# A Strassen product for the second half of the tokens in a transformer-layer kernel, low parts on GpSimd, and paced loads

## The chip, the cores and the metric

The kernel runs on one core of a Trainium2 chip. Its engines work side by side, each through its own list of instructions in strict order: TensorE (PE in the profile; its weight loads are PEld), VectorE (DVE), ScalarE (ACT), GpSimd (POOL) and SyncE (SP), which here only issues DMA transfers. The metric is the device time of one execution in microseconds. Three runs of the kernel before took 1467.42 to 1470.21 us, median 1467.71.

## The reference

The kernel computes one transformer layer on x (1024 tokens x 1024 features, float32) and 256 memory tokens: token mixing by two kinds of attention heads, cross-attention into the memory, and a squared-ReLU MLP. Each step is normalised before and after and added to the residual. The change touches the cross-attention's output product, and the loads of the head outputs that feed the mixing's output product:

```python
    y = jnp.concatenate([rmsnorm(y_fox.reshape(B, S, D_FOX), g_fox_out[l]),
                         rmsnorm(y_chk.reshape(B, S, D_CHK), g_chk_out[l])], axis=-1)
    x = x + rmsnorm(y @ w_out[l], g_mix_post[l])
    h = rmsnorm(x, g_mem_pre[l])
    mem_n = rmsnorm(mem, g_mem_kv[l])
    y = memory_cross_attention(h, mem_n, w_mq[l], w_mk[l], w_mv[l], w_mo[l])   # (P V) reshaped @ w_mo
    x = x + rmsnorm(y, g_mem_post[l])
    h = rmsnorm(x, g_ff_pre[l])
    y = jnp.square(jax.nn.relu(h @ w_ff1[l])) @ w_ff2[l]
```

## The kernel before

**High and low parts.** Every float32 operand of a product is split into a high part (ACT copies it into the matmul's type) and a low part (a subtraction, on DVE mostly). `mm3` (L191) makes one product of three matmuls: high x high, high x low, low x high. A weight block is loaded into a raw tile (tag `wraw`, three buffers), split into the tags `whi` and `wlo` (home "w", two buffers), into `wq` (one further pair) or into general tiles `u4` (30 buffers), and used.

**The planner.** From the attention to the middle of the cross-attention the order of all instructions is written by a planner, `Flow` (L56). Steps of TensorE stand in several streams. In each round the first stream whose next step is ready gives its matmuls; work for ACT ("S"), DVE ("V"), GpSimd ("G") and SyncE ("D") is put into waiting lists with a start time, a cost and a level, and the lowest level that is due goes first. The planner's costs and landing times are guesses written into the code: a load takes 0.55 us on SyncE's queue and lands `took` us later, and work that needs it is planned for that moment. The chip then runs the lists in that order and waits wherever a guess was too short.

**Head outputs.** Each attention head stores its output in DRAM (`od`, L761, through two buffers `o`). `Outputs.one` (L1009) loads them back as `oin`, four tiles of 128 x 512 for each half of the tokens (`th`) and group of heads (`g`), L1044. ACT and DVE split them into yT_hi and yT_lo (L1038, L1039), and `mix_steps` (L1174) multiplies them by w_out. For g = 0 the loads of both halves are issued together with a landing time of 7.0; for g = 1 it is 4.0.

**Cross-attention.** `query_steps`, `memory_score_steps`, `memory_turn_steps` and `memory_out_steps` (L1411) run for both halves of the tokens, head by head. For the first half (th = 0) the output product with w_mo is made by Strassen's algorithm (Winograd's form) in `strassen_steps` (L1443): the 512 x 1024 x 1024 product is cut into 256-token and 512-feature blocks, and seven block products stand for eight. `operand_tiles`, `operand_parts` and `sum_parts` make the sums of blocks of the head outputs (A11, A12, A22, S1 to S4) with high and low parts; the sums of weight blocks (T1 to T4) are made once by `Sums` (L1088) and kept in DRAM (`td`). `strassen_leave` (L1484) adds the products up in the rows y. Its weight pairs are given the homes "w", "w", "wq" in turn. For the second half (th = 1) the product is plain: `product_steps` (L1530) makes the left 512 columns inside the planner, with four weight pairs in "w", and the right 512 columns are made behind the planner, in the part written by hand.

**The turn.** Behind the planner comes an order by hand (L1986 on). The four row blocks of the second half are finished: right half of the product (24 matmuls a row block), `row_out`, `row_sum`, `row_norm` (L1970 to L1984). Beside them stand the first feed-forward products `ahead(j)` (L1891, 24 matmuls each, weights split by `split_ahead`, L1883). `Turn` (L1914) transposes the normalised rows on TensorE (`turn`), makes the block sums of the feed-forward's own Strassen product (`sums`) and their low parts (`low`): T2, T1, T3, T4 and B22. Before the manual part GpSimd makes eight sums `xf` (L1907) of the first half's parts.

Of the kernel before, what the change touches and what calls it, by code (L numbers as in the profile page):

```python
# [55 lines left out]
class Flow:  # L56
# [18 lines left out]
    def load(self, at, call, then=None, took=4.5):  # L75
        self.put("D", at, 0.55, call, then and (lambda end: then(end + took)))
# [59 lines left out]
def build(ctx, tc, nc, out, t):  # L136
# [249 lines left out]
    class Stock:  # L386
# [3 lines left out]
        def __init__(self):  # L390
# [602 lines left out]
    class Outputs:  # L993
# [15 lines left out]
        def one(self, th, g):  # L1009
# [20 lines left out]
            for i in range(2):  # L1030
                for j in range(2):
# [12 lines left out]
                    flow.load(flow.now, lambda o=o, kc=kc: nc.sync.dma_start(o, od[kc][th]), loaded, 7.0 - 3 * g)  # L1044
# [291 lines left out]
    def operand_tiles(h):  # L1336

        k = h % 2
        if h < 2:
            opt["r", k] = u4(f"ro{k}", (P, 2, HT), F32)  # L1340
            spent["r", k] = all_of(("r spent", k), 2, free["u4"].give)
        for n in ("A11",) if h < 2 else ("A12", "A22"):
            opt[n, k] = u4(f"{n}o{k}", (P, 2, 2, Q))
        if h == 0:
            opt["S3"] = u4("S3o", (P, 2, 2, Q), F32)
            for n, i in [(n, i) for n in ("S1", "S2", "S3", "S4") for i in range(2)]:
                parts_of[n, i] = all_of(("all", n, i), 3, lambda at, n=n, i=i: sum_parts(n, i, at))
            hi_tiles(("S3",))
        if h == 2:
            opt["S4"] = u4("S4o", (P, 2, 2, Q), F32)  # L1350
            spent["S4"] = all_of(("S4 spent",), 2, free["u4"].give)

    def operand(n, i):

        return opt[n, i][:, 0], opt[n, i][:, 1]

    def sum_parts(n, i, at):
        x = opt[n][:, i] if n in ("S3", "S4") else opt["r", i][:, :, Q:] if n == "S1" else opt["r", i][:, :, :Q]
        hi, lo = operand(n, i)

        def then(end):
            seen["A", n, i] = end
            if n != "S3":
                spent["S4" if n == "S4" else ("r", i)](end)
# [4 lines left out]
    def hi_tiles(names):  # L1369

        for n in names:
            for k in range(2):
                opt[n, k] = u4(f"{n}o{k}", (P, 2, 2, Q))
                parts_of[n, k](flow.end)
# [3 lines left out]
    def operand_parts(h, nb, ps):  # L1378

        k = h % 2  # L1380
        L, R = (opt["r", k][:, nb, c] for c in (slice(0, Q), slice(Q, HT)))
        left = lambda at: free["pv"].give(at)
        if nb == 0:
            lows[h] = all_of(("A", "A11" if h < 2 else "A12", k), 2)
            lows[h, 1] = all_of(("A", "A22", k), 2)
        if h < 2:
            ah, al = opt["A11", k][:, 0, nb], opt["A11", k][:, 1, nb]
            s3 = opt["S3"][:, k, nb]
            flow.put("S", flow.end, 0.6, lambda: nc.scalar.activation(opt["r", k][:, nb, :], ps, AF.Copy),
# [3 lines left out]
                         flow.put("V", at, 0.42, lambda: nc.vector.tensor_sub(s3, L, R), parts_of["S3", k])))  # L1393
            return
        hi, lo = ([opt[n, k][:, x, nb] for n in ("A12", "A22")] for x in range(2))
        s4 = opt["S4"][:, k, nb]
        halves = (ps[:, :Q], ps[:, Q:])
        gone = all_of(("out read", h, nb), 2, left)

        def block(x, then, level):  # L1400
# [7 lines left out]
                   lambda at: (gone(at), [parts_of[n, k](at) for n in ("S2", "S1", "S4")]), 0)  # L1408
        block(1, lambda at: (gone(at), lows[h, 1](at)), 1)

    def memory_out_steps():  # L1411
        for th in range(2):
            for h in range(4):
                done = all_of(("o", th, h), 2)
                for nb in range(2):
                    yield 1.362, lambda: there(("pt", th, h, 0), ("pt", th, h, 1)) and free["pv"].ready() \
                        and (nb or free["u4"].ready(2 if th else OPERANDS[h]))
                    if nb == 0:
                        for _ in range(2 if th else OPERANDS[h]):
                            free["u4"].take()  # L1420
                        if th:
                            outs[th, h] = u4(f"oT_hi{th}{h}", (P, 2, HT)), u4(f"oT_lo{th}{h}", (P, 2, HT))
                        if not th:
                            operand_tiles(h)
# [6 lines left out]
                    if not th:  # L1431
                        operand_parts(h, nb, ps)
                        continue
                    oh, ol = (x[:, nb, :] for x in outs[th, h])
                    flow.put("S", flow.end, 0.6, lambda oh=oh, ps=ps: nc.scalar.activation(oh, ps, AF.Copy),
                             lambda at, oh=oh, ol=ol, ps=ps, done=done: flow.put(
                                 "V", at, 0.7, lambda: nc.vector.tensor_sub(ol, ps, f(oh)),
                                 lambda end: (free["pv"].give(end), done(end))))
# [4 lines left out]
    def strassen_steps():  # L1443
# [4 lines left out]
        for p, (an, bn) in enumerate(PRODUCTS):  # L1448
            for i in range(2):
                for b in range(2):  # L1450
                    def room():
# [5 lines left out]
                    yield (1.362, lambda: there(("mo", 0, bn, i), ("A", an, i)) and (i or (  # L1457
                        there(("sum", before, b)) if goes_on else room())))
# [1006 lines left out]
```

## Time and profile before

| what | value |
|---|---|
| median of three runs | 1467.71 us |
| profiled execution, its own time | 1468.91 us |
| span of that execution | 1467.1 us |
| granted TensorE clock, mean | 0.998 |
| TensorE busy | 1450.2 us |
| VectorE busy | 997.1 us |
| ScalarE busy | 822.0 us |
| GpSimd busy | 420.4 us |
| DMA moved | 232.17 MB, mean 158 GB/s |

Times in the profile are microseconds from the start of the span; "mean ns" is the mean duration of one instruction. Instructions on one engine overlap: the next starts before the one ahead has ended, so what an instruction costs an engine is read from starts that stand back to back, not from its duration. A bracket behind a row tells how long the engine was idle before it and what ended that. A row with x8 merges eight instructions that follow each other. SPq is SyncE's queue. In a row of a stretch (two times with a colon) stand the length, the busy times of PE, PEld, DVE, ACT and POOL with their counts, the granted clock, the share of the DMA engines, and GB/s. The output product of the first half runs from about 679 to 728 us, that of the second half from 795.4 to 845.8, the turn from there to about 888.

### The profile page before, as it was taken

Reading aid. Unit: us, or ns where it says so; the run is one execution under the profiler, and the core shown is the slowest. Engines: PE = TensorE matmul, PEld = TensorE weight load, DVE = VectorE, ACT = ScalarE, POOL = GpSimd, SP = SyncE. Lnnn points to the kernel's source line nnn. Section 1 sums busy time; section 2 is a strip of 40 time slices with the busy share of each in tenths; the row PEclk is TensorE's granted clock in tenths of the full one; section 3 lists DMA queues with packets and bytes.
Section 4 is the critical chain, followed back from the end, with each engine's and each line's share of the span. In section 5 each row is a group of like instructions: output and inputs, shape, how many; then the busy total and the mean of one; then the engine's idle time right before and its main releaser. Section 6 shows DMA issues by size and latency. Waiting matters only on the chain.

```text
span 1467.1 us, 21030 instructions
## 1 busy us (share of the span) xinstructions
PE 1450.2 (99%) x7265; PEld 1223.0 (83%) x7265; DVE 997.1 (68%) x1704; ACT 822.0 (56%) x1439; POOL 420.4 (29%) x518
## 2 busy tenths in 40 slices
PE   9999999999999999999999999999999999999997
PEld 8988888888889788888788888888888888888886
DVE  6787777767668756975874687765555666655576
ACT  7567777666677736555553455545555543444442
POOL 1245456545445201531231413343222000000020
PEclk9999999999999999999999999999999999999999
DMA  7132324321326494552541547764444785445565
GB/s 274 48 98 72 79 69 139 83 83 46 92 62 172 152 331 150 170 190 81 178 157 44 186 143 248 241 221 158 144 156 167 283 319 180 139 150 191 187 244 201
DMA packets 88986, 232.17 MB, mean 158 GB/s; under 512 B 10648, under 2 KB 14752, under 8 KB 88880
## 3 DMA queue, kind: packets, MB, share of 16 engines
q1 hardware_dynamic: 88736, 230.57, 47.8%
q8 instruction: 57, 0.93, 0.3%
q14 instruction: 49, 0.40, 0.1%
q10 hardware_dynamic: 144, 0.26, 0.1%
HBM read 167.30 MB, written 55.11 MB: 152 GB/s over the span
## 4 chain that ended last, share of the span: by engine, by line
PE 92%; DMA 3%; DVE 2%; ACT 1%; issue 1%; SPq 0%; POOL 0%; DVEq 0%; ACTq 0%; POOLq 0%
PE pv L754 4%; PE fx L194 4%; PE fx L193 4%; PE fx L195 4%; PE ptr L711 4%; PE px L195 3%; PE px L194 3%; PE fy L193 3%; PE fy L194 3%; PE px L193 3%; PE fy L195 3%; PE q L193 2%; PE mq L195 2%; PE q L195 2%; PE q L194 2%; PE pz L193 2%
## 5 line engine op out<-in xcount | busy, mean ns | idle before, releaser
L717 DVE TENSOR_TENSOR phl<-ptr,phl 128x512 fp32r<-128x512 f32 (+1 forms) x152 | 92.5, 616 | 31.8 <-ACT phl L720 31.0
L2162 ACT ACTIVATE whif<-ra 128x1024 fp32r<-128x1024 f32 x37 | 39.2, 1061 | 130.4 <-PE fy L194 62.6
L2164 DVE TENSOR_TENSOR wlof<-ra,whif 128x1024 fp32r<-128x1024 f32 x37 | 45.3, 1225 | 91.8 <-ACT whif L2162 91.8
L720 ACT ACTIVATE phl<-ptr 128x512 fp32r<-128x512 f32 (+1 forms) x152 | 79.8, 540 | 40.7 <-PE ptr L711 38.8
L2284 POOL TENSOR_SCALAR rf<-sf 128x1 f32<-128x1 f32 x7 | 7.9, 1129 | 321.7 <-ACT jf L2265 321.4
L754 PE MATMUL pv<-phl,vs 128*128 128x512 f32 (+1 forms) x304 | 85.3, 366 | 3.0 <-DVE phl L717 3.0
L754 PEld LDWEIGHTS pv<-phl,vs 128*128 128x128 f32 x304 | 55.0, 188 | 14.4 <-DVE phl L717 4.2
L768 POOL TENSOR_TENSOR o<-o 64x256 f32<-64x256 f32 x64 | 47.0, 734 | 68.6 <-DVE o L766 50.0
L195 PE MATMUL fx<-vhif,wlof 128*128 128x512 f32 x168 | 65.4, 389 | 0.0
L193 PE MATMUL fx<-vhif,whif 128*128 128x512 f32 x168 | 65.4, 389 | 0.0
L194 PE MATMUL fx<-vlof,whif 128*128 128x512 f32 x168 | 65.4, 389 | 0.0
L2049 POOL TENSOR_TENSOR sc<-wf,wf 128x512 f32<-128x512 f32 x14 | 21.5, 1535 | 142.1 <-DMA wf<-in_w_ff 97.6
L766 DVE TENSOR_TENSOR o<-pv,o 64x512 f32<-64x512 f32 x64 | 44.0, 688 | 18.2 <-ACT o L771 16.9
L193 PE MATMUL k<-hT_hi,whik 128*128 128x512 f32 x128 | 53.6, 419 | 0.0
L193 PE MATMUL yw<-whiwo,yT_hi 128*128 128x512 f32 x128 | 51.1, 399 | 2.0 <-ACT yw L1196 2.0
L193 PE MATMUL q<-hT_hi,whiq 128*128 128x512 f32 x128 | 51.6, 403 | 0.0
L193 PE MATMUL mq<-h2T_hi,whimq 128*128 128x512 f32 x128 | 51.2, 400 | 0.0
L194 PE MATMUL yw<-wlowo,yT_hi 128*128 128x512 f32 x128 | 50.6, 396 | 0.0
L771 ACT ACTIVATE o<-pv 64x512 f32<-64x512 f32 x64 | 38.0, 593 | 22.4 <-issue 6.4
L195 PE MATMUL yw<-whiwo,yT_lo 128*128 128x512 f32 x128 | 50.4, 394 | 0.0
L195 PE MATMUL k<-hT_hi,wlok 128*128 128x512 f32 x128 | 50.3, 393 | 0.0
L195 PE MATMUL mq<-h2T_hi,wlomq 128*128 128x512 f32 x128 | 50.1, 392 | 0.2 <-DVE wlomq L455 0.2
(696 smaller groups left out, 5034.3 us busy)
## 6 DMA issues: line engine op xcount, KB each, us to landing
ra<-gd SPq DMA_DIRECT2D x56, 512.0 KB, 3.9
wg<-in_w_ff SPq DMA_DIRECT2D x56, 512.0 KB, 5.6
wf<-in_w_ff SPq DMA_DIRECT2D x38, 512.0 KB, 3.9
gd<-s SPq DMA_DIRECT2D x48, 256.0 KB, 2.1
wrawmq<-in_w_mq SPq DMA_DIRECT2D x16, 512.0 KB, 3.9
gd<-u SPq DMA_DIRECT2D x32, 256.0 KB, 2.4
gd<-g SPq DMA_DIRECT2D x25, 256.0 KB, 2.2
wrawq<-in_w_qk SPq DMA_DIRECT2D x8, 512.0 KB, 4.8
```

Of the source, the lines that this page charges most:

```text
L193: nc.tensor.matmul(ps, lh, rh, start=start, stop=False, skip_group_check=more)
L194: nc.tensor.matmul(ps, lh, rl, start=False, stop=False, skip_group_check=more)
L195: nc.tensor.matmul(ps, ll, rh, start=False, stop=stop, skip_group_check=more)
L711: nc.tensor.transpose(tr[:, m, :], sp[:, k * P:(k + 1) * P], ident)
L717: flow.put("V", at, 0.7, lambda: nc.vector.tensor_sub(pl[:, live, :], tr[:, live, :], f(ph[:, live, :])), done)
L720: flow.put("S", flow.end, 0.6, lambda ph=ph, tr=tr, live=live: nc.scalar.activation(ph[:, live, :], tr[:, live, :], AF.Copy), split)
L754: nc.tensor.matmul(pv[:, :, qs_, :], v, hl[:, :, hs, :], start=c == 0 and turn == 0, stop=last)
L766: flow.put("V", at, 0.7, lambda: nc.vector.tensor_add(o2[own], pv[own, :, :, ::step], o2[own]), lambda end: (free["pv"].give(end), flow.pu ...
L768: free["pv"].give(end), flow.put("G", end, 0.8, lambda: nc.gpsimd.tensor_add(o2[own, 0], o2[own, 0], o2[own, 1]), store)))
L771: flow.put("S", flow.end, 0.6, lambda: nc.scalar.activation(o2[own], pv[oth, :, :, ::step], AF.Copy), both)
L2162: nc.scalar.activation(ah, ra, AF.Copy)
L2164: nc.vector.tensor_sub(al, ra, f(ah))
```

## The change

- The planner's `load` takes a level. The loads of the head outputs are put at level 1, behind other loads that are due. For g = 0 they start 1.6 us apart (the second half's from 6.4 us on). Their landing time is 6.0 for both groups.
- The second half's output product is Strassen's too. Its tables of operands, tiles and sums get `th` as a key. Its 14 weight pairs replace eight; ten of them have the home "w", and B22 and T4 (four pairs) go to `u4`.
- Products 1 to 5 of the second half run in the planner. The last two are made in the order by hand: the sixth goes on in the banks that the fifth left (`left_over`), the seventh into new ones. `row_out` now adds (or subtracts) the bank into the row before it squares and scales.
- `ahead(0)` stands in front of the first `turn`; `ahead(1)` and `ahead(2)` move up too, and the row sums and norms are placed anew.
- The residual rows are loaded into `u4` tiles, three of them at once.
- At the turn, the low parts of T3 and T4 and the second half of the low parts of the feed-forward weights from j = 3 on go from DVE to GpSimd.
- `product_steps` is gone.

```diff
-    def load(self, at, call, then=None, took=4.5):
-        self.put("D", at, 0.55, call, then and (lambda end: then(end + took)))
+    def load(self, at, call, then=None, took=4.5, level=0):
+        self.put("D", at, 0.55, call, then and (lambda end: then(end + took)), level)
...
-                self.blocks += [(("mo", th, nh, kp), row_pair(t["w_mo"], kp, nh), pair)
-                                for nh in range(2) for kp in range(4)] if th else [
-                    (("mo", 0, b, i), row_pair(t["w_mo"], where[b][0] + i, where[b][1]) if b in where else td[b][i], pair)
+                self.blocks += [
+                    (("mo", th, b, i), row_pair(t["w_mo"], where[b][0] + i, where[b][1]) if b in where else td[b][i], pair)
                     for _, b in PRODUCTS for i in range(2)]
...
-                    if b[0][:3] == ("mo", 1, 1):
+                    if b[0][:3] in (("mo", 1, "B22"), ("mo", 1, "T4")):
                         self.home[b[0]] = "u4"
...
-                    flow.load(flow.now, lambda o=o, kc=kc: nc.sync.dma_start(o, od[kc][th]), loaded, 7.0 - 3 * g)
+                    flow.load(flow.now + 1.6 * (kc % 4 + 4 * th) * (1 - g), lambda o=o, kc=kc: nc.sync.dma_start(
+                        o, od[kc][th]), loaded, 6.0 if g == 0 else 6.0, 1)
...
     def second_filler():
         yield from mix_steps(0)
         yield from mix_steps(1)
         yield from query_steps(0)
-        yield from strassen_steps()
+        yield from strassen_steps(0)
         yield from query_steps(1)
-        yield from product_steps(1, (0,))
+        yield from strassen_steps(1, 5)
...
-            was[j] = HiLo(raw, D, wp, "w", 2, f"a{j}").both(nc.vector)
+            h = was[j] = HiLo(raw, D, wp, "w", 2, f"a{j}")
+            if j < 3:
+                h.both(nc.vector)
+                return
+            h.split_hi()
+            for e, cs in ((nc.vector, slice(0, HT)), (nc.gpsimd, slice(HT, D))):
+                e.tensor_sub(h.lo[:, cs], raw[:, cs], f(h.hi[:, cs]))
...
-            return lambda: nc.vector.tensor_sub(l, s, f(h))
+            return lambda: (nc.gpsimd if n in ("T3", "T4") else nc.vector).tensor_sub(l, s, f(h))
...
     def residual_in(b):
-        xts[b] = p2.tile([P, D], F32, tag="xt", bufs=2, name=f"xth3{4 + b}")
+        xts[b] = u4(f"xth3{4 + b}", (P, D), F32)
         nc.sync.dma_start(xts[b], x1d[4 + b])

     def row_out(b, ps):
-        square_sum(ps, ss[b][:, 1:2], HT)
-        nc.vector.tensor_tensor(y[b][:, HT:], ps, gmpost[:, HT:], op=ALU.mult)
+        cs = slice(HT, D) if b < 2 else slice(0, HT)
+        c, n = y[b][:, cs], cs.start // HT
+        if b < 2:
+            nc.vector.tensor_add(c, ps, c)
+        else:
+            nc.vector.tensor_sub(c, c, ps)
+        square_sum(c, ss[b][:, n:n + 1], HT)
+        nc.vector.tensor_tensor(c, c, gmpost[:, cs], op=ALU.mult)
         rx[b] = inverse_rms(ss[b][:, 0:1], f"h3y{4 + b}", ss[b][:, 1:2])
...
-    residual_in(0)
     raws = {}
-    for b in range(4):
-        c = slice(b * P, (b + 1) * P)
-        ps = mm_tile([P, HT], f"ym11{b}", "tr" if b < 2 else "pv")
-        for kp in range(4):
+    for b in range(3):
+        residual_in(b)
+
+    def last_product(b):
+        an, bn = PRODUCTS[5 if b < 2 else 6]
+        ps = left_over[4, b] if b < 2 else mm_tile([P, HT], f"ym16{b}", ("tr", "pv")[b % 2])
+        c = slice(b % 2 * P, (b % 2 + 1) * P)
+        for i in range(2):
+            (oh, ol), (wh, wl) = operand(1, an, i), stock.w["mo", 1, bn, i]
             for j in range(2):
-                mm3(ps, o[kp][0][:, j, c], o[kp][1][:, j, c], wo[kp][0][:, j, :], wo[kp][1][:, j, :],
-                    kp == 0 and j == 0, kp == 3 and j == 1)
-        if b:
-            row_sum(b - 1)
-            row_norm(b - 1)
-        if b < 3:
-            raws[EARLY + b] = ff1_raw(EARLY + b)
-            residual_in(b + 1)
-            row_out(b, ps)
+                mm3(ps, oh[:, j, c], ol[:, j, c], wh[:, j, :], wl[:, j, :],
+                    b > 1 and i == 0 and j == 0, i == 1 and j == 1, b < 2)
+        return ps
...
+    row_out(0, last_product(0))
+    raws[EARLY] = ff1_raw(EARLY)
+    row_out(1, last_product(1))
+    residual_in(3)
+    row_sum(0)
+    last = last_product(2)
+    raws[EARLY + 1] = ff1_raw(EARLY + 1)
+    row_sum(1)
+    row_out(2, last)
+    row_norm(0)
+    last = last_product(3)
+    row_norm(1)
+    row_out(3, last)
+    add[0] = ahead(0)
+    raws[EARLY + 2] = ff1_raw(EARLY + 2)
+    row_sum(2)
+    add[0]()
     units[0].turn()
-    row_out(3, ps)
     units[0].sums()
-    add[0] = ahead(0)
+    add[1] = ahead(1)
     row_sum(3)
+    row_norm(2)
     units[0].low()
-    add[0]()
     row_norm(3)
+    add[1]()
     units[1].turn()
-    units[1].sums()
-    add[1] = ahead(1)
     p2s.close()
...
-    add[1]()
     split_ahead(3, raws.pop(3))
+    units[1].sums()
+    add[2] = ahead(2)
     units[1].low()
     raws[6] = ff1_raw(6)
-    add[2] = ahead(2)
     units[2].turn()
```

More of the change, by code (lines that the diff above doesn't have):

```diff
@@ L1349, in operand_tiles @@
         if h == 2:
[L1350 to L1359, printed above, removed]
+            opt[th, "S4"] = u4(f"S4o{th}", (P, 2, 2, Q), F32)
+            spent[th, "S4"] = all_of(("S4 spent", th), 2, free["u4"].give)
@@ L1413, in memory_out_steps @@
             for h in range(4):
-                done = all_of(("o", th, h), 2)
                 for nb in range(2):
                     yield 1.362, lambda: there(("pt", th, h, 0), ("pt", th, h, 1)) and free["pv"].ready() \
-                        and (nb or free["u4"].ready(2 if th else OPERANDS[h]))
+                        and (nb or free["u4"].ready(OPERANDS[h]))
                     if nb == 0:
-                        for _ in range(2 if th else OPERANDS[h]):
+                        for _ in range(OPERANDS[h]):
                             free["u4"].take()
[L1421 to L1424, printed above, removed]
+                        operand_tiles(th, h)
                     free["pv"].take()
@@ L1456, in strassen_steps @@
                     goes_on = p in (2, 5)
-                    yield (1.362, lambda: there(("mo", 0, bn, i), ("A", an, i)) and (i or (
-                        there(("sum", before, b)) if goes_on else room())))
+                    yield (1.362, lambda: there(("mo", th, bn, i), ("A", th, an, i)) and (i or (
+                        there(("sum", th, before, b)) if goes_on else room())))
                     if not i:
@@ L1782, in build @@
     gmpost, gffpre = gains["memo"], gains["ff"]
-    o = [outs[1, h] for h in range(4)]
     y, ss = ys["m", 1]
```

137 lines of the change are left out of this document (50 added, 87 removed).

## The prediction

> **What bounds the kernel.** I read the page's engine totals first, then what TensorE waited for, then the timeline at its two longest waits, then busy time by stage.
>
> ```profile
> span 1467.1 us, 21030 instructions
> PE 1450.2 (99%) x7265; PEld 1223.0 (83%) x7265; DVE 997.1 (68%) x1704; ACT 822.0 (56%) x1439; POOL 420.4 (29%) x518
> ...
> PE pv L754 <- DVE phl L717: 3.0, 2, 2.9
> PE yw L193 <- ACT yw L1196: 2.0, 1, 2.0
> ...
> PE ym L193 <- ACT junk L1071: 0.4, 1, 0.4
> ```
>
> TensorE is busy 1450.2 of 1467.1 us. So a change helps by taking matmuls away or by closing a gap, and it hurts as soon as another engine makes TensorE wait. The list of waits has two gaps worth naming, 2.9 and 2.0 us. The profiled execution took 1468.91 us, 1.8 more than its span and 1.2 more than the median of the runs, 1467.71; my sum is made against 1468.9.
>
> **Part 1, fewer matmuls.** The second half's product has three groups of 64 matmuls, 192. Strassen with seven products of 256 tokens x 512 x 512 has 7 x 2 x 2 x 2 x 3 = 168.
>
> ```profile
> L193 PE MATMUL ym<-whimo,oT_hi 128*128 128x512 f32 x64 | 25.0, 394 | 0.1
> L194 PE MATMUL ym<-wlomo,oT_hi 128*128 128x512 f32 x64 | 25.0, 390 | 0.0
> L195 PE MATMUL ym<-whimo,oT_lo 128*128 128x512 f32 x64 | 24.9, 390 | 0.0
> ...
> 537.62 0.39 PE L193 MATMUL yw<-whiwo,yT_hi 128*128 128x512 f32 x1
> ...
> 540.34 0.39 PE L193 MATMUL yw<-whiwo,yT_hi 128*128 128x512 f32 x1
> ```
>
> The 390 ns of one overlap its neighbours: the two yw rows are twelve matmuls apart and 2.72 us apart, 0.227 each. Saved: 24 x 0.227 = **5.4 us**, not 9.4. All of it is on the path.
>
> **Part 2, the paced loads.** This is where the first gap comes from (timeline, SyncE's queue and the engines):
>
> ```profile
> 485.15 4.21 SPq L1044 DMA_DIRECT2D oin<-od  x8
> 489.73 1.13 SPq L761 DMA_DIRECT2D od<-o  x2
> ...
> 494.86 0.59 ACT L771 ACTIVATE o<-pv 64x512 f32<-64x512 f32 x1 [6.08 <-DMA od<-o]
> ...
> 498.15 1.16 DVE L717 TENSOR_TENSOR phl<-ptr,phl 128x512 fp32r<-128x512 f32 x2
> ...
> 498.90 1.09 PE L754 MATMUL pv<-phl,vs 128*128 128x512 f32 x4 [2.85 <-DVE phl L717]
> ```
>
> Eight loads of 256 KB go out in one block of 4.21 us. The stores od<-o queue behind them, ACT sits 6.08 us for their buffer, the split of phl behind it is late, and TensorE stands 2.85 us. After the change the first four loads leave 1.6 us apart and the second four from 6.4 us on, and at level 1, so stores and weight loads that are due go first. A store then stands behind one or two loads. I take all **2.85** (between 0, if another transfer takes the block's place, and 2.85); the next thing that could be late is the product's own weights wrawmv, which the same block held back, so they come earlier too.
>
> ```profile
> 544.29 2.34 SPq L1044 DMA_DIRECT2D oin<-od  x4
> ...
> 550.00 0.72 ACT L1038 ACTIVATE yT_hi<-oin,gcol 128x512 fp32r<-128x512 f32 x1 [5.29 <-DMA oin<-od]
> 550.63 0.67 ACT L1196 ACTIVATE yw<-yw,rs 128x512 f32<-128x512 f32 x1
> ...
> 551.35 0.50 PE L193 MATMUL yw<-whiwo,yT_hi 128*128 128x512 f32 x1 [2.01 <-ACT yw L1196]
> ...
> 551.00:553.00 2.00, 1.65 (x5) 1.33 (x6) 2.00 (x4) 2.00 (x5) 0.00 (x0) 0.79 1.05 405
> 553.00:555.00 2.00, 2.00 (x6) 1.62 (x5) 1.24 (x3) 2.00 (x5) 0.00 (x0) 0.50 1.05 406
> ```
>
> In the second gap the planner expected these loads 4 us after issue; ACT stood 5.29 us in front of yT_hi while the bank copy yw, planned just behind it, was ready. The new figure is 6.0, 2 us more, and the copies are 2.72 us apart, so one copy moves in front of yT_hi. The stage rows (the columns behind the engines are granted clock, DMA share, GB/s) show the rest of the price: a clock of 0.79 and 0.50 after the gap. Four us at those shares lose 0.42 + 1.0, and the tail about 0.2: 1.6. I take **2.0 + 1.6 = 3.6** (0 to 3.6). What is late next is the second half's head outputs, and they are not needed before mix step 1. The Trainium skill ("TensorE: Matmul & The Clock Gate", section "Why this matters for your kernels") asks for no idle gap above about 3 us. By that rule the 1.6 would not belong to this gap; the trace shows the slow clock right behind 2.01 us, and the row decides.
>
> **Part 3, what Strassen adds to the other engines.** Six more weight pairs (14 for 8): six loads of 512 KB on SyncE's queue, six ACT splits, six DVE splits. They use the two "w" buffers alone, where the first half's had a third pair ("wq").
>
> ```profile
> L449 ACT ACTIVATE whimo<-wrawmo 128x1024 fp32r<-128x1024 f32 x8 | 8.2, 1052 | 1.6 <-PE ym L195 1.6
> ...
> 701.06 0.42 DVE L1402 TENSOR_TENSOR A12o<-mo,A12o 128x256 fp32r<-128x256 f32 x1
> 701.39 0.42 DVE L1406 TENSOR_TENSOR ro<-ro 128x256 f32<-128x256 f32 x1
> ...
> 710.89 1.22 DVE L455 TENSOR_TENSOR wlomo_T<-wrawmo_T,whimo_T 128x1024 fp32r<-128x1024 f32 x1
> 712.02 0.69 DVE L1500 TENSOR_TENSOR ym<-ym,ym 128x512 f32<-128x512 f32 x1
> 712.63 1.28 DVE L1519 TENSOR_TENSOR ym<-ym,ym 128x512 f32<-128x512 f32 x2
> ...
> 832.16 1.28 DVE L1977 SCALAR_TENSOR_TENSOR xth<-ym,h3y,xth 128x1024 f32<-128x1024 f32 x1 [0.25 <-POOL h3y L1079]
> 833.37 1.22 DVE L1847 TENSOR_TENSOR wlo_a<-wf,whi_a 128x1024 fp32r<-128x1024 f32 x1
> ```
>
> By starts, back to back, DVE needs 0.33 us for 256 columns, 0.61 for 512, 1.13 for a 1024 split, 1.21 for a row operation. A weight half serves 12 matmuls, 2.72 us. Refilling its buffer takes 1.05 (ACT) + 1.22 (DVE) = 2.3, so 0.4 us is spare per half and one 0.61 operation in front uses it up. The first half's products, on three pairs, lost only the 0.4 us of the ym wait above.
>
> So DVE has to be counted by stage, from the last head output (810.5) to the first transposes (845.8), and on to the first feed-forward products (887.8):
>
> ```profile
> 810.50:824.00 13.50, 13.50 (x61) 11.20 (x60) 8.60 (x8) 6.29 (x10) 6.90 (x5) 1.00 0.52 153
> 824.00:836.00 12.00, 12.00 (x54) 9.93 (x54) 8.85 (x9) 7.89 (x15) 2.12 (x5) 1.00 0.69 218
> 836.00:845.80 9.80, 9.80 (x45) 8.06 (x44) 6.03 (x6) 2.77 (x5) 4.43 (x6) 1.00 0.83 278
> 845.80:866.00 20.20, 20.20 (x103) 16.99 (x102) 17.12 (x24) 13.06 (x25) 4.45 (x6) 1.00 0.29 106
> 866.00:887.80 21.80, 21.77 (x100) 17.82 (x99) 19.86 (x30) 11.99 (x20) 0.00 (x0) 1.00 0.54 173
> ...
> 805.39 12.01 POOL L1907 TENSOR_TENSOR xf<-h3T_hi,h3T_lo 128x512 f32<-128x512 f32 x8
> 814.48 5.14 DVE L455 TENSOR_TENSOR wlomo<-wrawmo,whimo 128x1024 fp32r<-128x1024 f32 x3 [1.13 <-ACT whimo L449]
> 893.04 1.28 POOL L2050 TENSOR_TENSOR wfu<-wfu 128x512 f32<-128x512 f32 x1
> ```
>
> First stage: before, DVE is busy 8.60 + 8.85 + 6.03 = 23.5 of 35.3 us. TensorE's time there stays 35.3, because ahead(0), 24 matmuls, now goes in front of the first transposes in place of the 24 saved. DVE's list becomes nine weight splits 10.2, three feed-forward splits 3.4, ten 256-column operand parts 3.4, twenty-one 512 operations 12.8 (five S parts, two, four and four for products 2 to 4, six for three last rows) and four row operations 4.8: 34.6. GpSimd's xf sums run until 817.4; beside them three splits took 5.14, 1.71 each for 1.13, so four splits lose 2.3. DVE: 36.9 in 35.3. Cost **1.6** (0 if the splits get ahead of need, 6 if every one of six halves of products 2 to 4 is held by a 1.13 operation less its 0.4 spare, 4.4, and the 1.6 comes on top).
>
> The last product's start: it adds into product 4's banks, so it waits for DVE's add of those banks. The cover is the other bank's six matmuls, 1.36; the need is 0.69 plus up to 1.22 for an operation in front, 1.9. I take **0.3** (0 to 0.6). The row chain from row 1's bank (add, square, gain, root, sum, square, root, norm) to the first transposes keeps its cover: before, two blocks of 24 matmuls, 10.9 us; now two last products of 12, 5.4, and ahead(0), 5.4. ACT, 13.06 of 20.2 in the fullest of these rows, hides its share.
>
> **Part 4, the turn.** Eight T3/T4 low parts of 0.61 and four half splits of 0.55 leave DVE, 7.1; a subtraction and a row sum that come later now add 1.8. Before, 17.12 + 19.86 = 37.0 of 42.0; after, 31.7 in 42.0 - 5.4 = 36.6. GpSimd takes 12 x 1.28 = 15.4, hidden in its own idle time (4.45 of 42), but DVE pays: by the 1.71 for 1.13 it loses a third of the time beside it, 5.2 if all of it lies beside two-SBUF work, half if half does. I take 4.0, and 2.5 of the 5.0 us that DVE idled there for the row chain: 38.2 against 36.6, cost **1.6** (0 to 13, third rival). A gain: TensorE waits from 882.30 + 0.23 to 882.72 for a split's low part; only its first half is needed there, and that comes sooner: **-0.2**. The residual loads move to the front of SyncE's queue into u4 buffers, past the raw feed-forward loads, which ahead(3) is the first to use, behind three blocks of 5.4 us: 0.
>
> ```profile
> 882.30 0.39 PE L194 MATMUL px<-h3T_lo,whi_a 128*128 128x512 f32 x1
> 882.72 0.50 PE L195 MATMUL px<-h3T_hi,wlo_a 128*128 128x512 f32 x1
> ```
>
> **Sum.** -5.4 - 2.85 - 3.6 - 0.2 + 1.6 + 0.3 + 1.6 = -8.5. 1468.9 - 8.5 = 1460.4; from the median, 1459.2. I say **1460**.
>
> **Rivals.** (a) *DVE eats the Strassen part.* Both stages are at 100% of DVE by my count, and a queue in strict order does not run at 100%. At 97% efficiency another 2.2 us goes: -6.3, about 1462.5. For: 36.9 in 35.3. Against: the first half's products ran as tight and lost 0.4.
> (b) *DVE costs nothing:* -12.0, 1457. For: the planner lays splits into gaps. Against: the two buffers.
> (c) *The gaps move.* Pacing changes every queue's order from 485 on, and the DMA share of 1.05 at 551 to 555 says that the transfers themselves are the limit; the waits return elsewhere. Then -5.4 - 0.2 + 3.5 = -2.1: 1466.8, no difference to be told.
> (d) *Slower: GpSimd shuts DVE out at the turn.* If every GpSimd operation holds DVE for its whole time, stage one needs 34.6 + 6.9 = 41.5 (+6.2) and stage two 31.7 + 15.4 + 2.5 = 49.6 (+13.0). Net -12.05 + 19.5 = +7.5: **1476**. It ends slower by 0.2% once DVE stands some 17 of GpSimd's 22.3 us. For: the 1.71 us splits. Against: they lost a third, not all. The Trainium skill ("SBUF — State Buffer", section "Who interferes with whom") states it as a rule: a VectorE instruction with two SBUF inputs contends with a GpSimd one that reads SBUF, and the loser blocks for the whole instruction. By it as a bound the sum is 1476; the trace agrees that they block, but by turns.
>
> **Chances.** Forecast 0.46 (1458 to 1462), (a) 0.16, (b) 0.12, (c) 0.14, (d) 0.12. A measurement here can tell 0.2%, 2.9 us: below 1464.8 is faster. Forecast, (a), (b) and 0.02 of (c) are faster, 0.76; the rest of (c) the same, 0.12; (d) slower, 0.12. The range 1455 to 1468 leaves out (d) and a little below (b).
>
> **What would show it.** 24 fewer ym matmuls; no wait over 1 us of pv on phl and of yw on its bank copy, and a clock of 1.00 around 550; SyncE's oin loads in singles; from the last head output to the first transposes TensorE within 2 us of 35.3 with DVE above 95%; 12 more GpSimd operations of 1.3 to 1.8 us at the turn. Wrong if TensorE's list of waits has a new entry above 2 us on a weight's low part or at the transposes, or if the two old ones stand.

## The result, and the profile after

The changed kernel took 1474.06 us (median of five runs, 1473.32 to 1476.37), beside 1468.52 for the kernel before on the same chip: a ratio of 1.0041, 95% interval 1.0029 to 1.0054. It is 0.4% slower; I had forecast 1460 and faster. The profiled execution took 1476.37 us, the slowest of the five and 2.3 above the median, with a span of 1474.6.

The page's totals, and the list of what TensorE waited for:

```profile
span 1474.6 us, 21083 instructions
...
PE 1449.4 (98%) x7241; PEld 1218.9 (83%) x7241; DVE 1023.8 (69%) x1740; ACT 834.8 (57%) x1463; POOL 444.1 (30%) x530
...
PE trx L1886 <- DVE y_m L1948: 4.1, 3, 2.7
PE px L195 <- DVE wlo_a L1848: 3.3, 4, 1.3
PE ym L193 <- DVE y_m L1508: 2.0, 1, 2.0
PE yw L193 <- ACT yw L1197: 1.4, 1, 1.4
...
PE ym L194 <- DVE wlomo_T L454: 1.3, 1, 1.3
```

The 24 matmuls are gone (7265 to 7241) and so is the 2.9 us wait for phl; that of yw shrank from 2.0 to 1.4. Four new waits stand in the list, every one on VectorE, whose busy time rose by 26.7 us. Two events, of the kernel before and of the kernel after, bound the place. The first pair is the third Strassen product of the first half's tokens, well behind the paced loads; the second pair is the first feed-forward product behind the turn:

```profile
705.87 0.50 PE L193 MATMUL ym<-whimo_T,S2o 128*128 128x512 f32 x1 [0.44 <-ACT junk L1071]
...
887.84 0.39 PE L193 MATMUL px<-T_hi,v0hi_s 128*128 128x512 f32 x1
```

```profile
700.50 0.50 PE L193 MATMUL ym<-whimo_T,S2o 128*128 128x512 f32 x1 [0.44 <-ACT junk L1072]
...
894.76 0.50 PE L193 MATMUL px<-T_hi,v0hi_s 128*128 128x512 f32 x1
```

The paced loads bring 5.4 us by 700.5. From there to the feed-forward products the kernel before needs 182.0 us and the one after 194.3, where 182.0 - 5.4 = 176.6 was to be had. What was lost lies in this stretch; behind it both are the same (579.3 and 579.8 us to the end). Busy time by stage, from the last head output to the first transposes and on to the feed-forward, is to be held against the stages that the prediction shows:

```profile
809.70:849.90 40.20, 35.16 (x146) 27.77 (x144) 34.77 (x44) 20.93 (x35) 12.44 (x13) 0.96 0.61 214
849.90:894.80 44.90, 40.22 (x177) 30.97 (x177) 39.95 (x48) 24.00 (x42) 25.33 (x19) 0.96 0.44 154
```

VectorE goes from 23.5 to 34.8 us of work in the first stage and from 37.0 to 40.0 in the second. Neither time reaches the length of its stage, and still TensorE waits in both. The first stage is 4.9 us longer than before (40.2 for 35.3), although some eleven matmuls of it (2.5 us) now run ahead of it. The second is 8.3 us longer than the 36.6 us that 24 fewer matmuls would leave of 42.0. The other 4.6 us of the loss stand ahead of the first stage: those eleven matmuls, and short waits, the longest of 1.27 us for a low part (wlomo_T). Three places show how (timelines of VectorE, TensorE, SyncE's queue and GpSimd, in order of time):

```profile
801.90 2.30 DVE L454 TENSOR_TENSOR wlomo_T<-wrawmo_T,whimo_T 128x1024 fp32r<-128x1024 f32 x1
...
815.41 1.21 DVE L454 TENSOR_TENSOR wlomo_T<-wrawmo_T,whimo_T 128x1024 fp32r<-128x1024 f32 x1
816.54 0.68 DVE L1508 TENSOR_TENSOR y_m<-ym,g_mem_post 128x512 f32<-128x512 f32 x1
...
817.28 0.50 PE L193 MATMUL ym<-whimo_T,S2o 128*128 128x512 f32 x1 [1.97 <-DVE y_m L1508]
...
818.77 0.63 PE L195 MATMUL ym<-whimo_T,S2o 128*128 128x512 f32 x1
...
831.39 4.43 SPq L1785 DMA_DIRECT2D wf<-in_w_ff  x2
835.87 0.42 SPq L1926 DMA_DIRECT2D xth<-x1d  x1
...
842.01 1.28 DVE L1941 SCALAR_TENSOR_TENSOR xth<-y_m,h3y,xth 128x1024 f32<-128x1024 f32 x1 [2.48 <-DMA xth<-x1d]
...
874.36 1.75 POOL L1848 TENSOR_TENSOR wlo_a<-wf,whi_a 128x512 fp32r<-128x512 f32 x1
```

First, a split that takes 1.22 us alone takes 2.30 beside GpSimd's xf sums. VectorE runs late from there on: a low part for product 1 comes 1.27 us late, and product 2 waits 1.97 us until VectorE, busy with a split, has read a bank (y_m, L1508). Behind that gap the matmuls last 0.63 instead of 0.39 us for some 3 us. Second, the residual loads stand on SyncE's queue behind two raw feed-forward loads that take 4.43 us to issue, and the first row sum waits 2.48 for them; the transposes wait 4.1 in all. The first of these loads lands some 6 us after its issue, where the DMA engines are 0.77 to 1.03 busy. Of the 4.43 us, 3.7 are a wait for VectorE's weight split, so this place, too, hangs on VectorE in part (from the list of what SyncE's queue waited for between 780 and 905; the longest one is the last number):

```profile
SPq L1785 <- DVE wlomo_T L454: 3.9, 2, 3.7
```

Third, half a split takes GpSimd 1.75 us at the turn, and TensorE waits four times for wlo_a. Each looked like a cause of its own.

### The profile page after: what moved, and what is told of

Its sections match the earlier page's. It is cut to its first block, busy times and chain, and to the rows that moved or that the text cites. A ratio compares the mean times of both kernels' runs of the same rounds, so it can differ in the third digit from the quotient of the medians.

```text
span 1474.6 us, 21083 instructions
## 1 busy us (share of the span) xinstructions
PE 1449.4 (98%) x7241; PEld 1218.9 (83%) x7241; DVE 1023.8 (69%) x1740; ACT 834.8 (57%) x1463; POOL 444.1 (30%) x530
## 4 chain that ended last, share of the span: by engine, by line
PE 87%; DVE 5%; DMA 3%; ACT 2%; issue 2%; POOL 1%; SPq 0%; DVEq 0%; ACTq 0%; POOLq 0%
PE pv L753 4%; PE fx L194 4%; PE fx L195 4%; PE fx L193 4%; PE ptr L710 4%; PE fy L194 3%; PE fy L195 3%; PE fy L193 3%; PE px L195 3%; PE px L193 3%; PE px L194 3%; PE k L193 2%; PE q L193 2%; PE q L194 2%; PE q L195 2%; PE k L194 2%
## 5 line engine op out<-in xcount | busy, mean ns | idle before, releaser
L194 PE MATMUL k<-hT_lo,whik 128*128 128x512 f32 x128 | 50.2, 393 | 0.0
L195 PE MATMUL q<-hT_hi,wloq 128*128 128x512 f32 x128 | 50.2, 392 | 0.0
L194 PE MATMUL q<-hT_lo,whiq 128*128 128x512 f32 x128 | 50.2, 392 | 0.0
```

The costliest lines, as they stand in the source:

```text
L194: nc.tensor.matmul(ps, lh, rl, start=False, stop=False, skip_group_check=more)
L195: nc.tensor.matmul(ps, ll, rh, start=False, stop=stop, skip_group_check=more)
```

## The experiments

My theory at the start (A): pacing brings its gain, and the three places above lose it again, each by itself, so that each can be repaired. Rivals: pacing delays other loads and loses what it gains (C); GpSimd shuts VectorE out at the turn (D, my rival (d)); VectorE simply has too much to do, whatever is repaired (B). The later letters are explained where they come.

Times against the kernel before are given as the ratio less one times 1468 us, with the same interval, since the kernel before varied by up to 1.3 us between the groups of runs. On this scale the changed kernel stands at **+6.0** (4.3 to 7.9).

**Pacing alone, and all but pacing.** In the kernel before, and left out of the kernel after:

```diff
-                    flow.load(flow.now, lambda o=o, kc=kc: nc.sync.dma_start(o, od[kc][th]), loaded, 7.0 - 3 * g)
+                    flow.load(flow.now + 1.6 * (kc % 4 + 4 * th) * (1 - g), lambda o=o, kc=kc: nc.sync.dma_start(
+                        o, od[kc][th]), loaded, 6.0 if g == 0 else 6.0, 1)
```

> The kernel before with the paced loads of head outputs and nothing else. Theory A (the loss lies in the Strassen part and the turn, three separate places): the gap at phl goes (2.85), the one at the bank copy yw shrinks (2.0 to 1.4) and the slow clock behind it goes; everything behind is as before, so 5.4 us less than before: 1463.1 against 1468.5, ratio 0.9963. Theory C (pacing pushes other loads, and what it gains is lost later): within 1.5 us of before, 1467 to 1470.

Measured: 1462.85 us, ratio 0.9961 (0.9946 to 0.9976), -5.7 us. The stretch around the second gap, in the kernel before and with pacing alone:

```profile
520.00:560.00 40.00, 37.99 (x169) 31.18 (x167) 20.39 (x29) 17.77 (x26) 1.02 (x1) 0.96 0.92 338
```

```profile
520.00:560.00 40.00, 39.43 (x178) 32.22 (x177) 19.11 (x27) 16.69 (x25) 1.01 (x1) 1.00 0.93 338
```

TensorE gains 1.44 us there, and the clock stays at 1.00. Theory A holds, C falls.

> The changed kernel with the loads of head outputs as they were before: Strassen for the second half and the turn alone. Theory A: the two gaps come back and nothing else changes, 1474.1 + 5.4 = 1479.5, ratio to before 1.0075. Theory C: the late residual loads and the late weights are the work of the paced loads, and without them the Strassen part gains its 5.4: about 1463 to 1468.

Measured: 1480.45 us, ratio 1.0084 (1.0067 to 1.0102), +12.3. Theory A again: pacing is worth 6 us in both kernels, and everything else in the change costs about 12. The paced loads alone are the version that beats both kernels.

**The low parts at the turn back on VectorE.**

```diff
-            h = was[j] = HiLo(raw, D, wp, "w", 2, f"a{j}")
...
-                e.tensor_sub(h.lo[:, cs], raw[:, cs], f(h.hi[:, cs]))
+            was[j] = HiLo(raw, D, wp, "w", 2, f"a{j}").both(nc.vector)
...
-            return lambda: (nc.gpsimd if n in ("T3", "T4") else nc.vector).tensor_sub(l, s, f(h))
+            return lambda: nc.vector.tensor_sub(l, s, f(h))
```

> The changed kernel with the low parts of T3 and T4 and the second halves of the splits of wlo_a back on VectorE. Theory A: the two engines cost each other at the turn as much as the offload saves, so within 1.5 us of the changed kernel (1472.6 to 1475.6), T_lo back at 0.6 to 0.7 us and the steps between the units still about 7.2 us. Theory D (GpSimd shuts VectorE out, my fourth rival, is where the loss is): the steps fall by 1 to 2 us each and the time by 5 to 8: 1466 to 1469. If VectorE's count is the bound: 7.1 us more work there, up to 1481.

Measured: 1474.36 us, 1.0037 (1.0022 to 1.0052), +5.4: no difference. VectorE has eight instructions more (1748) and is busy 1025.0 us, 1.2 more. GpSimd is busy 19.1 us less.

**The offload alone, on the kernel before.** The same lines, the other way round.

> The kernel before with the offload at the turn alone: T3's and T4's low parts and the second halves of four wlo_a splits on GpSimd. Theory A (the two engines cost each other what is saved): VectorE's busy time in the turn falls by less than 2 of the 7.1 us moved, the time stays within 1.5 us of before, 1466.8 to 1469.8. Theory D (GpSimd shuts VectorE out): VectorE's busy time grows, TensorE waits for wlo_a by over 2 us in all, 1471 or more. My own sum: -0.2.

Measured: 1469.64 us, 1.0016 (1.0006 to 1.0026), +2.3. VectorE's low parts and splits at the turn, before and with the offload alone, and GpSimd's low parts there (groups by shape: busy time, mean ns):

```profile
L1939 DVE TENSOR_TENSOR T_lo<-xf,T_hi 128x512 fp32r<-128x512 f32 x8 | 5.5, 688 | 0.0
...
L1847 DVE TENSOR_TENSOR wlo_a<-wf,whi_a 128x1024 fp32r<-128x1024 f32 x4 | 4.9, 1221 | 0.3 <-ACT whi_a L1844 0.3
...
L1949 DVE TENSOR_TENSOR T<-trx,xf 128x512 f32<-128x512 f32 x4 | 2.8, 692 | 0.4
```

```profile
L1945 DVE TENSOR_TENSOR T_lo<-xf,T_hi 128x512 fp32r<-128x512 f32 x4 | 4.9, 1230 | 0.0
...
L1895 DVE TENSOR_TENSOR wlo_a<-wf,whi_a 128x512 fp32r<-128x512 f32 x4 | 4.8, 1204 | 0.3 <-ACT whi_a L1844 0.3
...
L1955 DVE TENSOR_TENSOR T<-trx,xf 128x512 f32<-128x512 f32 x4 | 2.8, 692 | 0.4
...
L1945 POOL TENSOR_TENSOR T_lo<-xf,T_hi 128x512 fp32r<-128x512 f32 x4 | 7.5, 1872 | 0.0
```

Half a split now takes VectorE 1204 ns, where the whole one took 1221; four low parts take 4.9 us where eight took 5.5. Over the whole run VectorE has eight instructions fewer and is busy 997.4 us in place of 997.1. The offload saves VectorE nothing. T, which reads one operand from TensorE's bank, is not slowed: 692 ns in both. The Trainium skill ("SBUF — State Buffer", "Who interferes with whom") says both things, that two SBUF inputs contend with a GpSimd instruction that reads SBUF and one does not; the rows agree. The time is a little more above the kernel before than theory A's 1.5 us; TensorE waits 0.8 us for one wlo_a. Theory D's growth of VectorE's busy time didn't come.

**The early residual loads.** The three loads are issued before the loop that loads and splits the first feed-forward weights.

```diff
+    for b in range(3):
+        residual_in(b)
     for j in range(EARLY):
         split_ahead(j, ff1_raw(j), j == 0)
...
-    for b in range(3):
-        residual_in(b)
```

> The changed kernel with the three residual loads issued on SyncE's queue ahead of the second and third raw feed-forward load instead of behind them. Theory A (the loads are late because the queue stands before a raw feed-forward load whose buffer is freed late): the wait of the first row sum for xth (2.48) goes, the waits of the transposes (2.69 and 0.86) and the clock of 0.93 behind them go: 3.5 + 1.8 = 5.3 us less than the changed kernel, 1468.8. Theory B (VectorE's count alone sets the pace here): the row sum starts earlier, but the transposes wait for VectorE all the same; less than 1.5 us is gained, 1472.6 or more.

Measured: 1473.32 us, 1.0032 (1.0020 to 1.0043), +4.7; 1.3 less than the changed kernel, within what can be told. The row sum no longer waits, and the transposes still wait 3.4 us in place of 4.1: the largest, 2.0, now at the second pair of rows. Theory A missed; the time lies where theory B had it.

**A third pair of weight buffers.**

```diff
-                    elif b[0][:2] != ("mo", 1):
+                    else:
                         self.home[b[0]] = ("w", "w", "wq")[turn % 3]
```

> The changed kernel with a third pair of weight buffers (the tag wq) for the second half's Strassen weights, as the first half has it. Theory A1 (two buffers make the weights late): the waits of 1.27 and 1.97 us in products 1 and 2 and the 1.9 us of slow clock behind the second go, 4 to 5 us less than the changed kernel: 1469 to 1470. Theory A2 (the splits themselves are slow, 2.30 instead of 1.22 us beside GpSimd's xf sums, and VectorE's queue is full from 810 on): another buffer doesn't help, less than 1.5 us is gained, 1472.5 or more.

Measured: 1473.86 us, 1.0046 (1.0031 to 1.0061), +6.8. A1 was right on the two waits (they are gone) and wrong on the time. GpSimd's xf sums, which start at 800 in the changed kernel, now wait until product 3 for one of VectorE's sums (S4o), presumably because their memory comes free later, and there they slow what VectorE does then (timelines of GpSimd and VectorE):

```profile
821.01 15.86 POOL L1866 TENSOR_TENSOR xf<-h3T_hi,h3T_lo 128x512 f32<-128x512 f32 x8 [22.58 <-DVE S4o L1368]
...
825.54 3.48 DVE L1489 TENSOR_TENSOR y_m<-y_m,g_mem_post 128x512 f32<-128x512 f32 x2
828.95 2.31 DVE L454 TENSOR_TENSOR wlomo_T<-wrawmo_T,whimo_T 128x1024 fp32r<-128x1024 f32 x1
```

TensorE waited 1.8 us for low parts (wlomo_T) there, and the transposes then waited 4.9 us. The loss had moved.

**Without the xf sums.** `nc.gpsimd.tensor_add(xf...)` becomes `nc.gpsimd.memset(xf[i, a], 0.0)`.

> The changed kernel with GpSimd's eight xf sums left out: the tiles are filled with zeros, so the feed-forward of the first half's tokens is wrong. It prices the contention. Theory A2 (GpSimd's sums beside the weight splits): the four slow splits fall from 2.3 to 1.2 us, VectorE gets 4.4 us back between 800 and 815, the waits of 1.27 and 1.97 shrink below 0.5 and the slow clock behind goes: 4 to 5 us less than the changed kernel, 1469 to 1470. Theory A1 (two buffers): the wait of 1.97 stays above 1.4, and 1473 or more. What lies behind (transposes, wlo_a) stays as it is in both.

Measured: 1472.65 us, 1.0032 (1.0019 to 1.0045), +4.7. The splits fell to 1.22 and 1.23 us (GpSimd only writes there) and VectorE's busy time by 5.7; the waits in products 1 and 2 fell to 0.8 in all. But the first row sum then waited 4.00 us for its residual load, and the transposes 5.1. VectorE had time to spare in front of the row sums, and the late load took it. A2 had the waits right and the time wrong.

**More cover in front of the transposes.** `ahead(1)` goes before `units[0].turn()`, and each later `ahead` and split moves by one place.

> The changed kernel with ahead(1) in front of the first transposes too, and the splits and sums around it moved by one block, so that TensorE has 5.4 us more to do while the four rows are finished. Theory E (the row chain has lost its cover, since the last four row blocks have 12 matmuls instead of 24): the waits of the transposes (4.1 us in all) and the 1.7 us of slow clock behind them go, and nothing comes in their place: 5 to 6 us less than the changed kernel, about 1468.5. Theory B (VectorE has more to do from the last product to the feed-forward products than TensorE has): the transposes wait less, but the feed-forward weights wlo_a and v0 come late by about as much; less than 1.5 us is gained, 1472.5 or more.

Measured: 1483.90 us, 1.0113 (1.0098 to 1.0128), +16.6. My order was at fault: whi_a stood on ACT's queue behind the high parts of the turn, which wait for VectorE.

```profile
PE px L193 <- ACT whi_a L1797: 12.3, 4, 4.0
```

```diff
     units[0].turn()
+    split_ahead(3, raws.pop(3))
     units[0].sums()
     add[2] = ahead(2)
-    split_ahead(3, raws.pop(3))
```

> e7_cover again with the splits of the feed-forward weights one place earlier on ACT's queue: there, their high parts stood behind the turn's own high parts and TensorE waited 12.3 us for them, which hid what was asked. ahead(1) stands in front of the first transposes. Theory E (lost cover of the row chain): the transposes' waits (4.1) and the 1.7 us of slow clock go, nothing comes in their place, 5 to 6 us less than the changed kernel, 1468 to 1469. Theory B (VectorE has more work than TensorE from here to the feed-forward products): wlo_a and the first v0 come late by as much, less than 2 us is gained, 1472 or more.

Measured: 1473.46 us, 1.0039 (1.0025 to 1.0053), +5.7. The transposes don't wait at all any more; wlo_a costs 3.3 us as before, and a new wait of 3.7 stands at v0, whose high part ACT copies from a sum that VectorE makes late (ACT waited 3.57 us for it). Theory B.

```profile
PE px L193 <- ACT v0hi_s L1797: 3.7, 1, 3.7
```

**Repairs together.** The third pair with the early loads, and then both with the new order and the low parts on VectorE.

> The changed kernel with the third pair of weight buffers and the early residual loads together. Alone they gained 0 and 0.7 us; with the third pair the waits in products 1 and 2 went, but the transposes waited 4.9 in place of 4.1 us. Theory F (the two stand in series, the one hides behind the other): together 4 to 5 us less than the changed kernel, 1469 to 1470. Theory B (VectorE's amount of work): the waits move on, to the transposes of the second pair of rows and to wlo_a; less than 2 us is gained, 1472 or more.

Measured: 1474.31 us, 1.0046 (1.0031 to 1.0061), +6.8; the transposes wait 4.8 us.

> All repairs at once: paced loads, Strassen for the second half with a third pair of buffers, early residual loads, ahead(1) in front of the transposes, low parts at the turn on VectorE. If the losses are separate waits (theories E and F), 11.5 us of waits and 3.5 of slow clock go but for the 3.8 at wlo_a: 1462 to 1464, no worse than the paced loads alone (1462.9). Theory B: VectorE needs about 84 us at its undisturbed durations between 795 and 895 for the 85 us of TensorE's work there, 5 more beside GpSimd's sums; some 5 us of waits stay, 1466 to 1470.

Measured: 1473.14 us, 1.0033 (1.0020 to 1.0046), +4.8. Even theory B, which I had at 1466 to 1470, was too mild. Forty microseconds of the turn:

```profile
855.00:895.00 40.00, 33.75 (x147) 25.84 (x146) 38.92 (x53) 23.68 (x40) 6.70 (x6) 0.96 0.50 175
```

VectorE is busy 38.92 of 40 us and TensorE 33.75: there is next to no idle time of VectorE left that a repair could use.

**GpSimd's twelve operations taken from both engines.** ACT copies stand in for them.

> The changed kernel with the twelve GpSimd operations at the turn taken from both engines: ACT copies in their place, and the subtraction of the high part is left out there. It prices the offload. Theory A (GpSimd's operations cost VectorE what they save): VectorE's T_lo, wlo_a halves and sums fall to 0.6 to 0.7 us, the waits for wlo_a and v0 (3.8 us) fall below 1, 3 to 4 us less than the changed kernel, 1470 to 1471. If the turn is bound by its chain of transposes, sums and splits and not by VectorE's work: within 1 us of the changed kernel.

Measured: 1472.84 us, 1.0030 (1.0019 to 1.0042), +4.4. T_lo and the halves of wlo_a fell to 681 to 687 ns, as theory A has it, but only 1.6 of 3 to 4 us came: whi_a was late by 1.9 us on ACT, to whose busy time the copies add 6.5 us, in place of wlo_a.

**VectorE's work taken out.** Three edits together: zeros for xf, ACT copies for the twelve operations, and no multiplication by the gain in the second half's rows; first in the changed kernel, then in the one with the repairs. The last run leaves out only the xf sums, with all repairs.

> The changed kernel with some 14 us of VectorE's time taken out and nothing repaired: xf filled with zeros on GpSimd, ACT copies for the twelve GpSimd operations of the turn (the subtraction left out), and the six multiplications by the gain left out in the second half's rows. Theory B (VectorE's amount of work from product 1 to the feed-forward products): the waits of TensorE fall from 11.6 us below 4 and the time by 9 to 12 us, 1462 to 1465. Theory G (a chain of late loads and row operations sets the transposes whatever VectorE has to do): products 1 and 2 and the wlo_a waits gain 5 to 6 us, the transposes' 4 to 6 us stay, 1468 to 1470.

> The same 14 us of VectorE's time taken out of the kernel with the repairs (third pair of buffers, early residual loads, ahead(1) in front of the transposes). Theory B: as e17_less, the repairs add at most 2 us: 1460 to 1465. Theory G: the repairs, useless while VectorE was full, now bring the transposes' 4 to 6 us: 1459 to 1462, at least 4 below e17_less.

> The kernel with all repairs (e12_all) with GpSimd's xf sums left out (zeros): what their contention costs there, where they had moved to 822 to 835 and eight VectorE operations filled 10 us. If VectorE's amount counts: its busy time falls by 5 us, and the time by 4 to 5: 1468 to 1469. If the waits move on to another cause: less than 1.5 us, 1471.6 or more.

Measured: e17_less 1466.73 us, 0.9992 (0.9982 to 1.0001), -1.2; e16_all_less 1460.42 us, 0.9948 (0.9933 to 0.9962), -7.6; e18_all_no_xf 1467.99 us, 1.0004 (0.9995 to 1.0014), +0.6. VectorE is busy 1006.7, 1007.1 and 1018.4 us in them. Against the kernel before:

| | repairs left out | repairs made |
|---|---|---|
| VectorE's work as it is | +6.0 (VectorE 1023.8 us) | +4.8 (1024.1 us) |
| some 17 us of it taken out | -1.2 (1006.7 us) | -7.6 (1007.1 us) |

The table tells the two apart. While VectorE is full, shortening the waits is worth 1.2 us, less than can be told; with its work out, the repairs are worth 6.4. Taking the work out gains 7.2 without the repairs and 12.4 with them. e17_less fell less than theory B had said and kept 3.0 us of waits at the transposes, and its time lies between the two ranges, so the chain of loads and rows is real as well; e16_all_less is 6.3 us below it, as theory G has it. In e16_all_less the turn looks like this, from the middle of the last products on:

```profile
835.00:865.00 30.00, 30.00 (x145) 24.73 (x144) 25.95 (x35) 22.93 (x41) 9.68 (x12) 1.00 0.74 249
```

TensorE 30.00 of 30. The xf sums alone, with the repairs, are worth 4.2 (+4.8 to +0.6), close to VectorE's 5.7 us. What each of the three pieces is worth in e16_all_less was not separated, and leaving out the gains also lets the planner order its work anew. The work that is left out is not quite the same in the two columns either: the twelve operations come off GpSimd on the left and off VectorE on the right. In both, the part of VectorE's time that GpSimd's xf sums cost it (5.7 us) goes with its own instructions, so the table shows what VectorE's time is worth, and not its instructions alone.

The 1460.42 us are close to my forecast, and no support for it: that kernel leaves out work that the layer needs. It is only 1.9 us ahead of the paced loads alone (-7.6 beside -5.7).

## Why the prediction was wrong

**Part 1** was right in the count (24 matmuls). The price of 5.4 us shows only in part: from the third Strassen product to the first feed-forward product e16_all_less needs 178.4 us and pacing alone 181.9, 3.4 less, and e16_all_less still waits some 2 us there.

**Part 2** was right: I had 6.45 us, and pacing measured 5.7 alone and 6.3 as the difference of two kernels. The first gap went whole. Of the second, 0.6 us (pacing alone) to 1.45 us (kernel after) stayed, with the clock at 1.00 in both. In the other kernels with paced loads 0.5 to 2.2 us stayed, so that the size of this gain is partly luck.

**Part 3** is where it failed, at the step "DVE: 36.9 in 35.3. Cost 1.6", which takes the longer of two nearly equal times as the length of the stage. The count was near: VectorE was busy 34.8 us there. But the stage took 40.2, a cost of 4.9, and that with eleven matmuls fewer than I had left in it. Part 4 takes the same step for the turn, 38.2 against 36.6; the turn took 44.9, a cost of 8.3 in place of 1.6. What the runs show in place of that overlap is two full engines that wait for each other: VectorE stood 2.48 us for a residual load and 1.65 us for ACT's high part of a weight, and TensorE then waited for what VectorE made late. My rival (a) had the idea and priced it at 97% efficiency; measured are 34.77 of 40.20, or 86%, and 39.95 of 44.90, 89%, in the turn. These shares came out of the runs and are no ceiling: in e12_all VectorE is busy 97% of 40 us. In the turn of the kernel before it was busy 36.98 of 42.0, 88%, while TensorE hardly waited. Had I divided my own counts, 36.9 and 38.2, by these 88%, the stages would have been 41.9 and 43.4 in place of 35.3 and 36.6: 13.4 us of cost, and with -5.4 - 6.45 - 0.2 + 0.3 a sum of +1.6, slower. That is near the result, but the row gave no reason for it. My own signs of being wrong both stand in the list of waits: 4.1 us at the transposes and 3.3 on a weight's low part (wlo_a).

**The residual loads at 0** were wrong: the row sum waited 2.48 us for them (4.00 where VectorE had less to do). I had looked at who uses the raw feed-forward loads, and not at what those loads themselves wait for on SyncE's queue. By itself the early issue was worth 1.3 us, within what can be told.

**"The row chain keeps its cover"** was wrong too: with the row blocks halved, the transposes waited 4.1 us. Another 5.4 us of cover ended that wait, and the time came back at v0.

**Part 4**: I took 7.1 us off VectorE and gave 4.0 back for contention. The runs gave it all back: eight instructions fewer, and 0.3 us more. The xf sums cost 2.3 in my sum; taking them out lowers VectorE's busy time by 5.7.

**Rival (d)** named 1476, near the result, by luck: with the twelve operations back on VectorE the time is the same, and without the xf sums the changed kernel is only 1.3 us faster. GpSimd does hold VectorE up, by 5.7 us with its xf sums, but the greater part of what filled VectorE is its own added work. Before, 1704 instructions took 997.1 us; with everything back on it, 1748 take 1025.0, 27.9 us more.

## What to carry to other kernels

Saving matmuls pays only where the engine that feeds them has room. When its counted work nearly equals the new length of the stage, don't take the longer of the two as the stage's time: here such stages ran at 86 and 89% of VectorE, and no single share holds for all (97% in a stretch of e12_all). When a repair only moves a wait, take some work out of the suspected engine in a run of its own, with and without the repairs; four runs help to tell a full engine from a chain. An operation given to GpSimd is worth what the other engine's rows get shorter by, and beside two-SBUF work here that was nothing.

## What the runs showed of the hardware that I had not expected

A 512-column subtraction of two SBUF tiles costs VectorE 1.2 to 1.8 us beside a GpSimd one, 0.69 alone, and GpSimd's own grows from 1.28 to 1.6 to 1.9 on average: both lose, so that here moving half of an operation made the other half as long as the whole (1204 ns beside 1221).

The clock doesn't fall behind every gap of the same length. The wait of 1.97 us in front of product 2 stands in the kernel after and again in e7_cover. The 3.2 us behind it, in the one and in the other:

```profile
817.28:820.48 3.20, 3.20 (x10) 2.50 (x10) 3.20 (x5) 1.54 (x3) 0.00 (x0) 0.65 0.48 164
```

```profile
816.94:820.14 3.20, 3.20 (x13) 2.36 (x13) 3.20 (x5) 1.69 (x4) 0.00 (x0) 1.00 0.47 164
```

Behind this wait four kernels had a slow clock (the kernel after, e3_turn_dve, e4_resid_early, e10_cover2) and three a clock of 1.00 (e2_no_pace, e7_cover, e15_no_lows). Behind the gap of 2.85 us at phl in the kernel before, and behind one of 3.09 there in e9_offload_alone, it stayed at 1.00. A gap of 1.64 us at v0 (e18_all_no_xf), with one of 0.52 just behind it, was followed by 0.50 over 2 us. The Trainium skill ("TensorE: Matmul & The Clock Gate", "Why this matters for your kernels") warns of gaps above about 3 us; in these rows no length parts the gaps that cost clock from those that don't, and what does stays open. Where the clock fell behind the wait of 1.97 us (kernel after: 0.82, 0.50 and 0.70 over the next 1.5, 2 and 1.5 us), it cost some 1.7 us more; the same product in another kernel ran without that loss.
